# Sparse attention: scores from stacked split operands, with the causal mask as a matrix product and the keys spread by transfers

## The chip, the cores and the metric

One core of one Trainium2 chip runs the whole program. The metric is the time of one execution on the device, in microseconds (us). PE is TensorE (matrix products), DVE is VectorE, ACT is ScalarE, POOL is GpSimd, SP is SyncE, which here only issues loads of weights.

## What is computed

The program is a small network on 256 tokens of width 1024. Ten stages follow one another: a gated feed-forward block, an S5 mixer, two more feed-forward blocks, a convolution, a further feed-forward block, a retention layer, a mixture of experts by product keys ("peer"), a sparse attention ("nsa"), and a second peer. The change lies in the sparse attention alone. Cut to what matters, with 16 heads of 64 in 4 groups, so that four heads share keys and values:

```python
q = (h @ w_in)[..., :1024] * 64 ** -0.5
s = q . k_cmp                                  # coarse branch: 15 compressed keys
o_cmp = masked_softmax(s, end <= t) . v_cmp
s = q . k_slc ; o_slc = masked_softmax(s, tok <= t) . v_slc
s = q . k_win ; o_win = masked_softmax(s, kp <= t) . v_win
out = gate0 * o_cmp + gate1 * o_slc + gate2 * o_win
y = out @ w_o
```

With 256 tokens all blocks of 64 are selected and the window of 512 reaches over everything, so the second and the third branch are both full causal attention, with keys and values of their own.

## The kernel before, in words

Weights and activations are f32. A projection is done in three products of the type fp32r: each operand x is split into a high part (an ACT copy that rounds to fp32r) and a low part (DVE subtracts the high part), and high x high, high x low and low x high are added in PSUM (`mm3`, lines 281 to 283). Weights are loaded by SP, 1 MB each, into three buffers (`wload`, L247) and split by ACT and DVE (`wsplit`, L264, L265). The kernel uses eight PSUM banks: four under the tag "acc", two under "mm", two under "tr". Products outside the projections (scores, transposes, probabilities times values) take plain f32 operands.

The order of the instructions on each engine is made by a scheduler when the program is built: it takes what is ready by its own estimate of times, the earlier in the text first, and sets the waits. Work late in the text can so run early when its engine has nothing else; each engine then runs its list in order.

The stage `nsa` (L1395 to L1670) goes like this. Constants are loaded, among them the mask, [128, 2, 256]: 0 or -1e30 for each of two tiles of 128 queries. The values V of both branches are projected. Keys and values of the compressed branch go to `kv2` (L1427 to L1431), two copies for each of four groups, one of them a token ahead. Then `kT` (L1432 to L1442): for each branch b (two) the keys come from a projection into PSUM with two groups on the two row halves, and are copied, by ACT to rows 0 to 63 with zeros (POOL's memsets) in the other head slot, by DVE to rows 64 to 127 in the other slot. So one product of all 128 rows gives the scores of two heads side by side. `apply_pending` (L1444) finishes the layer norm of the stage before (eight DVE operations on 512 columns); the result is needed only at the end of this stage. The compression network follows (`nsfl`, L1458 to L1468), and the queries: `query(g)` (L1472 to L1475) projects four heads and copies them, scaled, into `qT`, two heads stacked on the row halves.

The attention loop (L1640 on) runs over 16 pairs of heads, eight pairs for the first query tile (one key tile of 128, so n = 128) and eight for the second (n = 256):

- `softmax(i)`: for both branches, one f32 product of q with `kT` into a bank "mm" (two heads x n columns, L1565); DVE adds the mask into `nssm` in SBUF (L1568); one DVE reduction over all gives the four negative maxima (L1571); ACT takes four exponentials in place, with their sums (L1574).
- `turn(i)`: PE transposes the probabilities (L1587), DVE and ACT copy them out (L1592, L1594).
- `attend(i)`: products with V (L1606), and after four pairs the scaling and summing into `o_sb`.

In the text `softmax` is two pairs ahead of `turn` and `attend`. `nssm` has three buffers. `coarse_softmax(qt)` and `coarse_out(qt)` do the compressed branch for a query tile; its scores are eight f32 products of 32 columns (L1515). Then come the output projection and the norm, and the next stage.

```python
def softmax(i):
    sm = nw.tile([P, 2, 2, S], F32, tag="nssm", bufs=3, ...)
    for b in range(2):
        sp = self.mm()
        nc.tensor.matmul(sp, lhsT=qT[:, g, fb, tile], rhs=kT[:, b, g, :, :n], start=True, stop=True)
        v.tensor_tensor(sm[:, b, :, :n], sp, mask[:, qt, :n], ALU.add)
    v.tensor_reduce(nm, sm[:, :, :, :n], AX.X, ALU.max, negate=True)
    ...
```

## Time and profile before

| what | us |
|---|---|
| median of 3 runs | 3199.64 (3199.46 to 3200.47) |
| the profiled execution | 3200.87 |
| its span, first to last instruction | 3199.1 |
| PE busy | 3120.6 |
| DVE busy | 2508.9 |
| ACT busy | 1567.3 |
| POOL busy | 105.0 |

The page of the profile gives busy time over the whole span. The stage `nsa` takes a small part of it, and is read in the views that take a stretch: a table by stretches, groups of instructions by line and shape, and a timeline. Product lengths on PE are pipelined (the next one starts before one has ended), so that their price is read from the distance of their starts.

### The profile page before, as it was taken

The page shows a single profiled execution, that of the slowest core. Times are in us where ns is not written, and L with a number is a line of the kernel's source. Part 1 is how long each engine was busy: PE and PEld are TensorE (multiplying, and loading weights), DVE is VectorE, ACT ScalarE, POOL GpSimd, SP SyncE. Part 2 cuts the span into 40 slices and gives each one's busy share as a digit, 9 for nine tenths or more (in the row PEclk, how much of TensorE's full clock was granted, in tenths as well). Part 3 has the DMA queues.
Part 4 walks back from the last instruction along what each step waited for, and adds up shares of the span by engine and source line. Part 5 has one row for each costly group of instructions (what it writes and reads, how often), then busy time and mean ns, then how long its engine had stood idle before and what let it go on. Part 6 is the DMA issues. An engine that isn't in the chain of part 4 may idle for free. (4 is left out here: it accounts for less than half of the span.)

```text
span 3199.1 us, 52281 instructions
## 1 busy us (share of the span) xinstructions
PE 3120.6 (98%) x20484; PEld 2829.5 (88%) x20484; DVE 2508.9 (78%) x4935; ACT 1567.3 (49%) x2350; POOL 105.0 (3%) x172
## 2 busy tenths in 40 slices
PE   8998999999999999999999999999999999999998
PEld 7888899898889888899999998888789999999887
DVE  8877867876986786899976666886789997666787
ACT  5556544446454443545654444335554665444432
POOL 1320000000000000000000000001000000000000
PEclk9999999999999999999999999999999999999999
DMA  5665767674266664445776666665044677566674
GB/s 212 209 230 184 290 228 278 242 287 146 89 242 244 251 250 169 168 153 200 231 255 214 215 215 212 228 226 194 32 159 160 206 235 258 201 215 215 211 239 163
DMA packets 174968, 668.36 MB, mean 209 GB/s; under 512 B 20705, under 2 KB 95233, under 8 KB 101762
## 3 DMA queue, kind: packets, MB, share of 16 engines
q1 hardware_dynamic: 150304, 606.05, 54.0%
q10 hardware_dynamic: 21826, 49.54, 4.1%
q0 software_dynamic: 2592, 9.44, 0.9%
q8 instruction: 161, 2.64, 0.3%
q14 instruction: 85, 0.70, 0.1%
HBM read 619.88 MB, written 45.11 MB: 208 GB/s over the span
## 5 line engine op out<-in xcount | busy, mean ns | idle before, releaser
L264 ACT ACTIVATE wh<-raw 128x1024 fp32r<-128x1024 f32 x948 | 998.5, 1059 | 1199.0 <-PE mm L282 617.6
L265 DVE TENSOR_TENSOR wl<-raw,wh 128x1024 fp32r<-128x1024 f32 x948 | 1150.1, 1221 | 403.9 <-ACT wh L264 392.9
L281 PE MATMUL mm<-xTh,wh 128*128 128x256 f32 x4032 | 1152.5, 286 | 4.5 <-ACT pg L1835 1.7
L283 PE MATMUL mm<-xTh,wl 128*128 128x256 f32 x4032 | 1142.5, 284 | 2.7 <-DVE wl L265 2.7
L282 PE MATMUL mm<-xTl,wh 128*128 128x256 f32 x4032 | 1144.5, 284 | 0.3 <-DVE xTl L355 0.3
L281 PEld LDWEIGHTS mm<-xTh,wh 128*128 128x128 f32 x4032 | 773.5, 192 | 15.7 <-ACT pg L1835 3.2
L282 PEld LDWEIGHTS mm<-xTl,wh 128*128 128x128 f32 x4032 | 773.6, 192 | 8.0 <-issue 0.7
L283 PEld LDWEIGHTS mm<-xTh,wl 128*128 128x128 f32 x4032 | 773.1, 192 | 4.7 <-DVE wl L265 4.4
L283 PE MATMUL acc<-wh,pal 128*128 128x512 f32 x1024 | 403.8, 394 | 0.0
L282 PE MATMUL acc<-wl,pah 128*128 128x512 f32 x1024 | 403.4, 394 | 0.0
L281 PE MATMUL acc<-wh,pah 128*128 128x512 f32 x1024 | 402.9, 393 | 0.0
L283 PEld LDWEIGHTS acc<-wh,pal 128*128 128x128 f32 x1024 | 192.6, 188 | 44.3
L281 PEld LDWEIGHTS acc<-wh,pah 128*128 128x128 f32 x1024 | 193.6, 189 | 39.3
L282 PEld LDWEIGHTS acc<-wl,pah 128*128 128x128 f32 x1024 | 192.7, 188 | 40.1
L1788 ACT ACTIVATE pwb<-tr 128x512 f32<-128x512 f32 x128 | 130.8, 1088 | 24.5 <-PE tr L1785 20.6
L281 PE MATMUL acc<-wh,gh 128*128 128x512 f32 x352 | 141.3, 402 | 0.0
L282 PE MATMUL acc<-wl,gh 128*128 128x512 f32 x352 | 139.8, 397 | 0.0
L283 PE MATMUL acc<-wh,gl 128*128 128x512 f32 x352 | 138.5, 399 | 0.3 <-DVE gl L405 0.3
L1781 DVE TENSOR_SCALAR poh<-pe_iota,pi,pwT 128x128 f32<-128x128 f32 x512 | 136.7, 338 | 0.0
L1849 DVE CAST pah<-pa 128x256 fp32r<-128x256 f32 x256 | 74.7, 293 | 69.6 <-PE acc L282 69.6
L1850 DVE TENSOR_TENSOR pal<-pa,pah 128x256 fp32r<-128x256 f32 x256 | 108.3, 424 | 25.3 <-DVE pah L1849 0.9
L1785 PE MATMUL tr<-poh,poh 128*128 128x128 f32 x1024 | 125.2, 275 | 1.6 <-ACT pwb L1788 1.6
(480 smaller groups left out, 3517.7 us busy)
## 6 DMA issues: line engine op xcount, KB each, us to landing
raw<-in_w SPq DMA_DIRECT2D x132, 1024.0 KB, 4.9
raw<-in_pe_u SPq DMA_DIRECT2D x128, 1024.0 KB, 4.8
raw<-in_pe_v SPq DMA_DIRECT2D x128, 1024.0 KB, 4.8
adaraw<-in_ada_w SPq DMA_DIRECT2D x48, 1024.0 KB, 6.9
pe_wscr<-pwb ACTq DMA_DIRECT2D x32, 1024.0 KB, 8.5
pwr<-pe_wscr SPq DMA_DIRECT2D x30, 1024.0 KB, 6.9
raw<-in_ret_vg SPq DMA_DIRECT2D x16, 1024.0 KB, 4.8
raw<-in_pe_wq SPq DMA_DIRECT2D x16, 1024.0 KB, 4.8
```

What stands on the lines that cost most here:

```text
L264: nc.scalar.activation(h, raw[:, sl], AF.Copy)
L265: nc.vector.tensor_sub(l, raw[:, sl], h.bitcast(F32))
L281: mm(out, lhsT=ah, rhs=bh, start=start, stop=False)
L282: mm(out, lhsT=ah, rhs=bl, start=False, stop=False)
L283: mm(out, lhsT=al, rhs=bh, start=False, stop=stop)
L1781: v.tensor_scalar(oh1[:, j, :], iota[:, :NK], i1[:, t:t + 1], wT[:, t:t + 1], ALU.is_equal, ALU.mult)
L1785: nc.tensor.matmul(ps[:, j * P:j * P + P], lhsT=oh2[:, t4 * 4 + j, :], rhs=oh1[:, t4 * 4 + j, :], start=True, stop=True)
L1788: nc.scalar.activation(wb[:, :, o:o + 4].rearrange("p i t -> p t i"), ps.rearrange("p (t i) -> p t i", t=4), AF.Copy)
L1849: v.tensor_copy(ah, a)
L1850: v.tensor_sub(al, a, ah.bitcast(F32))
```

## The change

- **Queries.** `qT` gets twice the room. For each head pair slot r (row half) ACT copies the scaled queries, rounded to fp32r, onto their own row half, and DVE writes the low part, scaled q minus high part, onto the other half. One column of 128 rows then holds a head's high and low part.
- **Keys.** The projected keys are split once over all 128 rows (`split_T`: one ACT copy, one DVE subtraction) into a high and a low part, and each of them is brought to both row halves by DMAs that POOL issues: 2 branches x 2 parts x 2 row halves read x 2 written, 16 of 128 KB. The copies and the memsets of `kT` go.
- **Scores.** For each head: queries x high keys (both branches side by side), then identity x mask on the last 128 keys of each branch, then queries x low keys, all fp32r and added in one PSUM bank. DVE reduces from PSUM; ACT's exponentials read PSUM and write SBUF.
- **Room.** `nssm` becomes three places: the two tiles of the stage's input (`new_T`, free after the last query) and one buffer. `kv2` lies in `o_sb`, which is written later.
- **Coarse scores**: sixteen fp32r products of 32 columns (high and low keys side by side) instead of eight f32 ones, and one more DVE addition.
- **Order.** `apply_pending` moves behind `query(1)`; `softmax(0)` moves ahead of `coarse_softmax(0)`. The mask shrinks to 128 x 128; ACT makes fp32r copies of it and of the identity.

```diff
-            mask, cmask = cload("ns_mask", [P, 2, S]), cload("ns_cmask", [P, 2, 2, 16])
+            cmask = cload("ns_cmask", [P, 2, 2, 16])
+            mask = np_.tile([P, P], F32, name="ns_mask")
+            nc.scalar.dma_start(out=mask, in_=self.I["ns_mask"][:, 0, :P])
...
-            kv2 = kp.tile([P, 2, 4, S], F32, name="ns_kv2")
+            kv2 = [o.rearrange("p h d -> p (h d)").rearrange("p (g t) -> p g t", g=4) for o in o_sb]
...
-            kT = np_.tile([P, 2, 4, 2, S], F32, name="ns_kT")
-            nc.gpsimd.memset(kT[0:64, :, :, 1, :], 0.0)
-            nc.gpsimd.memset(kT[64:128, :, :, 0, :], 0.0)
+            halves = [slice(0, 64), slice(64, 128)]
+            kT = [np_.tile([P, 4, 2, S], F32R, name="ns_kT" + i) for i in "hl"]
             for b in range(2):
                 ps = self.mm()
                 self.lin_b(xh, xl, self.I["ns_k"][b], ps)
-                for g in range(4):
-                    q = slice(64 * (g % 2), 64 * (g % 2) + 64)
-                    o = g // 2 * S
-                    nc.scalar.activation(kT[0:64, b, g, 0, :], ps[q, o:o + S], AF.Copy)
-                    v.tensor_copy(kT[64:128, b, g, 1, :], ps[q, o:o + S])
-
-            self.apply_pending()
+                parts = [nw.tile([P, 512], F32R, tag="nspT", bufs=4, name=self.nm("nsk")) for _ in range(2)]
+                self.split_T(ps, *parts)
+
+                for part, t in zip(parts, kT):
+                    for r, q in enumerate(halves):
+                        for d in halves:
+                            nc.gpsimd.dma_start(out=t[d, r::2, b, :], in_=part[q].rearrange("p (f t) -> p f t", f=2))
+
+            one = np_.tile([P, P], F32R, name="ns_one")
+            nc.scalar.activation(one, self.ident, AF.Copy)
+            low = np_.tile([P, 2, P], F32R, name="ns_low")
+            for b in range(2):
+                nc.scalar.activation(low[:, b, :], mask, AF.Copy)
...
-                nc.scalar.activation(qT[:, g].rearrange("p f t -> p (f t)"), ps, AF.Copy, scale=0.125)
+                for r, q in enumerate(halves):
+                    h, l = (qT[d, g, r].rearrange("p f t -> p (f t)") for d in (q, halves[1 - r]))
+                    nc.scalar.activation(h, ps[q], AF.Copy, scale=0.125)
+                    v.scalar_tensor_tensor(l, ps[q], 0.125, h.bitcast(F32), ALU.mult, ALU.subtract)
...
             query(1)
+            self.apply_pending()
...
-                for p in range(8):
-                    nc.tensor.matmul(cs[:, p * 32:p * 32 + 32], lhsT=qT[:, p // 2, p % 2, qt * P:qt * P + P],
-                                     rhs=kcT[:, p // 2].rearrange("p r n -> p (r n)"), start=True, stop=True)
+                for h in range(16):
+                    nc.tensor.matmul(cs[:, h * 32:h * 32 + 32], lhsT=qT[:, h // 4, h % 2, h % 4 // 2, qt * P:qt * P + P],
+                                     rhs=kcT[:, h // 4].rearrange("p i n -> p (i n)"), start=True, stop=True)
...
+                v.tensor_add(sc, sc, cs[:, :, 1, :])
...
+            rooms = [t.bitcast(F32).rearrange("p d t -> p (d t)")[:, :4 * S] for t in self.new_T()]
+            rooms.append(nw.tile([P, 4 * S], F32, tag="nssm", bufs=1, name=self.nm("nssm")))
...
-                sm = nw.tile([P, 2, 2, S], F32, tag="nssm", bufs=3, name=self.nm("nssm"))
-                for b in range(2):
-                    sp = self.mm()
-                    nc.tensor.matmul(sp[:, :2 * n].rearrange("p (r k) -> p r k", r=2),
-                                     lhsT=qT[:, g, fb, qt * P:qt * P + P],
-                                     rhs=kT[:, b, g, :, :n], start=True, stop=True)
-                    v.tensor_tensor(sm[:, b, :, :n], sp[:, :2 * n].rearrange("p (r k) -> p r k", r=2),
-                                    mask[:, qt, :n].unsqueeze(1).to_broadcast([P, 2, n]), ALU.add)
+                sm = rooms[i % 3]
                 nm = nw.tile([P, 2, 2], F32, tag="nsnm", bufs=3, name=self.nm("nsnm"))
-                v.tensor_reduce(nm, sm[:, :, :, :n], AX.X, ALU.max, negate=True)
                 for r in range(2):
+                    sp = self.mm()[:, :2 * n].rearrange("p (b k) -> p b k", b=2)
+                    q = qT[:, g, r, fb, qt * P:qt * P + P]
+                    nc.tensor.matmul(sp, lhsT=q, rhs=kT[0][:, g, :, :n], start=True, stop=False)
+                    nc.tensor.matmul(sp[:, :, n - P:], lhsT=one, rhs=low, start=False, stop=False)
+                    nc.tensor.matmul(sp, lhsT=q, rhs=kT[1][:, g, :, :n], start=False, stop=True)
+                    v.tensor_reduce(nm[:, r, :], sp, AX.X, ALU.max, negate=True)
                     for b in range(2):
-                        nc.scalar.activation(sm[:, b, r, :n], sm[:, b, r, :n], AF.Exp, bias=nm[:, b, r:r + 1],
+                        nc.scalar.activation(sm[:, b, r, :n], sp[:, b, :], AF.Exp, bias=nm[:, r, b:b + 1],
                                              accum_out=den[:, qt, 1 + b, h + r:h + r + 1])
...
-            coarse_softmax(0)
             softmax(0)
+            coarse_softmax(0)
             softmax(1)
```

## Rows read from the trace of the kernel before

**Rows 1.** The page, part 1: busy time of each engine over the span.

```profile
PE 3120.6 (98%) x20484; PEld 2829.5 (88%) x20484; DVE 2508.9 (78%) x4935; ACT 1567.3 (49%) x2350; POOL 105.0 (3%) x172
```

**Rows 2.** Table by stretches: each engine's busy us (instructions), PEclk, DMA share, GB/s.

```profile
2222.00:2248.00 26.00, 26.00 (x219) 25.81 (x216) 13.64 (x13) 15.69 (x21) 0.00 (x0) 1.00 0.66 243
...
2248.00:2320.00 72.00, 67.81 (x430) 53.85 (x428) 57.61 (x110) 42.48 (x154) 0.00 (x0) 1.00 0.04 15
```

**Rows 3.** Groups by shape, PE, 2181 to 2320: busy, mean ns | idle before, releaser.

```profile
L1565 PE MATMUL mm<-ns_kT,ns_qT 128*128 128x512 f32 x32 | 16.2, 600 | 0.3 <-DVE nssm L1568 0.2
...
L1565 PE MATMUL mm<-ns_kT,ns_qT 128*128 128x256 f32 x32 | 9.3, 399 | 1.2 <-DVE nssm L1568 1.1
```

**Rows 4.** Timeline of PE: start us, length us, instruction.

```profile
2245.00 0.28 PE L283 MATMUL mm<-xTh,wl 128*128 128x256 f32 x1
...
2245.12 0.28 PE L281 MATMUL mm<-xTh,wh 128*128 128x256 f32 x1
...
2301.96 1.88 PE L1565 MATMUL mm<-ns_kT,ns_qT 128*128 128x512 f32 x4
...
2303.68 1.89 PE L1606 MATMUL acc<-ns_V,nspT 128*128 128x64 f32 x16
...
2316.32 0.40 PE L282 MATMUL acc<-wl,oTh 128*128 128x512 f32 x1
...
2316.56 0.39 PE L283 MATMUL acc<-wh,oTl 128*128 128x512 f32 x1
```

**Rows 5.** Timeline of PE: the coarse products of the second query tile.

```profile
2255.70 1.87 PE L1515 MATMUL tr<-ns_kcT,ns_qT 128*128 128x32 f32 x16
```

**Rows 6.** Groups by shape, DVE: mask additions, reductions, and one out of PSUM (L1161).

```profile
L1568 DVE TENSOR_TENSOR nssm<-mm,ns_ns_mask 128x512 f32<-128x512 f32 x16 | 10.8, 684 | 2.3 <-PE mm L1565 2.0 <-PE tr L1587 0.2
...
L1571 DVE TENSOR_REDUCE nsnm<-nssm 128x4 f32<-128x1024 f32 x8 | 9.6, 1204 | 0.1
...
L1568 DVE TENSOR_TENSOR nssm<-mm,ns_ns_mask 128x256 f32<-128x256 f32 x16 | 6.4, 414 | 1.5 <-PE mm L1565 1.3
...
L1571 DVE TENSOR_REDUCE nsnm<-nssm 128x4 f32<-128x512 f32 x8 | 5.4, 678 | 0.1
...
L1161 DVE TENSOR_REDUCE adacol<-tr 128x4 f32<-128x512 f32 x28 | 18.2, 682 | 1.8 <-PE tr L1160 1.8
```

**Rows 7.** Groups by shape, ACT: exponentials, copies out of PSUM, the query copy.

```profile
L1574 ACT ACTIVATE nssm<-nssm,nsnm 128x256 f32<-128x256 f32 x32 | 15.8, 497 | 1.1 <-DVE nsnm L1571 1.0
...
L1574 ACT ACTIVATE nssm<-nssm,nsnm 128x128 f32<-128x128 f32 x32 | 12.4, 389 | 4.9 <-DVE nsnm L1571 4.9
...
L1594 ACT ACTIVATE nspT<-tr 128x256 f32<-128x256 f32 x8 | 3.0, 375 | 6.6 <-PE tr L1587 6.6
...
L1524 ACT ACTIVATE nssc<-nssc 128x256 f32<-128x256 f32 x2 | 0.8, 408 | 0.0
...
L1475 ACT ACTIVATE ns_qT<-mm 128x512 f32<-128x512 f32 x4 | 2.4, 588 | 1.0 <-PE mm L283 1.0
```

**Rows 8.** Instructions on the keys' tile: length ns (least, median, most), first and last start.

```profile
L1565 PE MATMUL mm<-ns_kT,ns_qT x64: 379/536/697, 2249.3 to 2308.8; 128*128 128x256 f32 x32, 128*128 128x512 f32 x32
...
L1441 ACT ACTIVATE ns_kT<-mm x8: 363/379/381, 2198.8 to 2209.3; 64x256 f32<-64x256 f32 x8
```

**Rows 9.** POOL's DMA issues; DMA sizes and us to landing; the stretch after the keys.

```profile
L312 POOL DMA_DIRECT2D rowbc<-in_ln_r x6 | 3.4, 568 | 621.8 <-ACT wh L264 619.1 <-ACT hT L340 2.8
...
rowbc<-in_ln_r POOLq DMA_DIRECT2D x6, 512.0 KB, 6.3
...
ns_cmp_w<-in_cmp_w ACTq DMA_DIRECT2D x1, 128.0 KB, 3.0
...
2199.00:2207.00 8.00, 8.00 (x72) 8.00 (x71) 3.65 (x9) 3.14 (x8) 0.00 (x0) 1.00 0.00 0
```

**Rows 10.** Table by stretches, columns as in rows 2: around an idle spot of PE.

```profile
2322.00:2324.00 2.00, 0.81 (x5) 0.61 (x5) 2.00 (x4) 1.65 (x2) 0.00 (x0) 1.00 0.03 8
...
2324.00:2326.00 2.00, 2.00 (x6) 1.58 (x5) 2.00 (x3) 2.00 (x3) 0.00 (x0) 0.52 0.00 0
```

More of the change, by code (lines that the diff above doesn't have):

```diff
@@ L1429, in nsa @@
                     o = g // 2 * S
-                    nc.scalar.activation(kv2[0:64, c, g, :], ps[q, o:o + S], AF.Copy)
-                    v.tensor_copy(kv2[64:128, c, g, 0:S - 1], ps[q, o + 1:o + S])
-            kT = np_.tile([P, 2, 4, 2, S], F32, name="ns_kT")
-            nc.gpsimd.memset(kT[0:64, :, :, 1, :], 0.0)
-            nc.gpsimd.memset(kT[64:128, :, :, 0, :], 0.0)
+                    nc.scalar.activation(kv2[c][0:64, g, :], ps[q, o:o + S], AF.Copy)
+                    v.tensor_copy(kv2[c][64:128, g, 0:S - 1], ps[q, o + 1:o + S])
+            halves = [slice(0, 64), slice(64, 128)]
+            kT = [np_.tile([P, 4, 2, S], F32R, name="ns_kT" + i) for i in "hl"]
             for b in range(2):
@@ L1448, in nsa @@
             nc.gpsimd.memset(hid, 0.0)
-            kcT = np_.tile([P, 4, 2, 16], F32, name="ns_kcT")
-            nc.gpsimd.memset(kcT, 0.0)
+            kcT = np_.tile([P, 4, 2, 16], F32R, name="ns_kcT")
+            nc.gpsimd.memset(kcT.bitcast(F32), 0.0)
             vc = np_.tile([P, 4, 64], F32, name="ns_vc")
@@ L1460, in nsa @@
                         fl = kp.tile([P, 4, 15], F32, tag="nsfl", bufs=4, name=self.nm("nsfl"))
-                        v.tensor_scalar(fl, kv2[:, c, :, 2 * lc:2 * lc + 225:16], pe[:, c, lc:lc + 1], None, ALU.add)
+                        v.tensor_scalar(fl, kv2[c][:, :, 2 * lc:2 * lc + 225:16], pe[:, c, lc:lc + 1], None, ALU.add)
                         for hb in range(2):
@@ L1469, in nsa @@
                                          AF.Gelu_apprx_tanh, bias=b1[:, c, hb:hb + 1])
-            qT = np_.tile([P, 4, 2, S], F32, name="ns_qT")
+            qT = np_.tile([P, 4, 2, 2, S], F32R, name="ns_qT")
             def query(g):
@@ L1486, in nsa @@
                 if c == 0:
-                    for half in range(2):
-                        nc.scalar.activation(kcT[64 * half:64 * half + 64, :, half, :15],
-                                             cp[:64, :P].rearrange("p (g n) -> p g n", g=4)[:, :, :15], AF.Copy)
+                    cpv = cp[:64, :P].rearrange("p (g n) -> p g n", g=4)[:, :, :15]
+                    for q in halves:
+                        nc.scalar.activation(kcT[q, :, 0, :15], cpv, AF.Copy)
+                    for q in halves:
+                        v.tensor_sub(kcT[q, :, 1, :15], cpv, kcT[:64, :, 0, :15].bitcast(F32))
                 else:
@@ L1513, in coarse_softmax @@
                 cs = self.tr()
-                for p in range(8):
-                    nc.tensor.matmul(cs[:, p * 32:p * 32 + 32], lhsT=qT[:, p // 2, p % 2, qt * P:qt * P + P],
-                                     rhs=kcT[:, p // 2].rearrange("p r n -> p (r n)"), start=True, stop=True)
+                for h in range(16):
+                    nc.tensor.matmul(cs[:, h * 32:h * 32 + 32], lhsT=qT[:, h // 4, h % 2, h % 4 // 2, qt * P:qt * P + P],
+                                     rhs=kcT[:, h // 4].rearrange("p i n -> p (i n)"), start=True, stop=True)
+                cs = cs.rearrange("p (h i n) -> p h i n", h=16, i=2)
                 sc = nw.tile([P, 16, 16], F32, tag="nssc", name=self.nm("nssc"))
                 sh = [P, 16, 16]
-                v.tensor_tensor(sc, cs[:, :S].rearrange("p (h n) -> p h n", h=16),
-                                cmask[:, 0, qt, :].unsqueeze(1).to_broadcast(sh), ALU.add)
+                v.tensor_tensor(sc, cs[:, :, 0, :], cmask[:, 0, qt, :].unsqueeze(1).to_broadcast(sh), ALU.add)
+                v.tensor_add(sc, sc, cs[:, :, 1, :])
                 mx = nw.tile([P, 16], F32, tag="nscm", name=self.nm("nscm"))
@@ L1555, in nsa @@
             pairs = [(qt, half, pr) for qt in range(NT) for half in range(2) for pr in range(4)]
+            rooms = [t.bitcast(F32).rearrange("p d t -> p (d t)")[:, :4 * S] for t in self.new_T()]
+            rooms.append(nw.tile([P, 4 * S], F32, tag="nssm", bufs=1, name=self.nm("nssm")))
+            rooms = [t.rearrange("p (b r k) -> p b r k", b=2, r=2) for t in rooms]
             def softmax(i):
@@ L1626, in nsa @@
             flat = [o.rearrange("p h d -> p (h d)") for o in o_sb]
+            softmax(0)
             coarse_softmax(0)
-            softmax(0)
             softmax(1)
```

## The prediction

> **What bounds the kernel now.** The page comes first: TensorE is busy 98% of the span, DVE 78%, ACT 49% [rows 1]. A busy PE is not yet PE at its peak, so the second view is the table by stretches. The change touches one stage, about 2181 to 2320 us. While the queries are projected (2222 to 2248) PE has no idle time, ACT 15.7 and DVE 13.6 us of work in 26. From there to 2320 PE is busy 67.8 of 72 us, so it idles 4.2, with DVE at 57.6 and ACT at 42.5 [rows 2]. PE therefore sets the time also in the attention loop, with DVE close behind. The third view, the groups by shape, says what the score products cost: 32 instructions of 512 columns and 32 of 256 (an f32 product is two instructions), and that PE idled 0.3 and 1.2 us before them, for DVE's mask additions [rows 3]. The mean of 600 ns there is a pipelined length and no price. The price is the distance of starts, in the timeline: four f32 instructions of 512 columns begin at 2301.96 and the next work at 2303.68, so 0.43 us each; one of 256 I take as half, 0.215. The products on split (fp32r) operands stand 0.235 us apart at 512 columns and 0.12 at 256; the small f32 products of the loop 0.118 (sixteen in 1.89) [rows 4].
>
> **The change part by part.**
> **Scores on PE.** Now: 32 x 0.43 + 32 x 0.215 = 20.6 us. After: for each of 16 pairs and 2 heads, two fp32r products and the mask product. With one key tile (8 pairs) all three have 256 columns: 48 x 0.12 = 5.8. With two (8 pairs) two have 512 and one 256: 16 x (2 x 0.235 + 0.12) = 9.4. Sum 15.2, so **5.4 us less PE work**. The products alternate weights as the projections behind [rows 4] do, so I see no reason for another price. Bounds: 4.4 (each of the 96 products 10 ns dearer) and 5.7.
> **Coarse scores.** Sixteen instructions per query tile take 1.87 us now [rows 5]; sixteen fp32r products of 32 columns replace them. At 0.117 each they are already at the distance of the small products, so 0, bounds -0.5 and +0.5. DVE gets one 256-wide addition more per tile, 2 x 0.41, beside PE.
> **DVE in the loop.** A pair now costs 2 x 0.684 + 1.204 = 2.57 us with two key tiles and 2 x 0.414 + 0.678 = 1.51 with one. After, two reductions out of PSUM: 512 wide from PSUM takes 0.682 where 512 from SBUF takes 0.678 [rows 6], so 1.36 and about 0.83. Over eight pairs each that is 15 us less of DVE. DVE is not the bound; only the waits that it causes count: 1.5 us of PE idle in [rows 3]. **I take -1.5**, bounds 0 and -2.7 (idle of 4.2 down to 1.5).
> **Exponentials out of PSUM.** ACT keeps 64 exponentials (0.389 at 128, 0.497 at 256). No row has the same one from PSUM; nearest are a copy of 256 from PSUM, 0.375, and an exponential of 256 from SBUF, 0.408, both without the sum [rows 7]. So I take no dearer, perhaps 0.03 cheaper. [...]
> What changes on the path is **how long a score buffer is held**. There are two PSUM buffers of this kind. Now each is free after DVE's addition. After, it is held until reduction and both exponentials are done, and what is queued behind it is everything on PE: next scores, then the product with V. With one key tile: after head 0's products, about 0.1 + 0.41 + 0.78 (head 0's exponentials) + 0.78 (head 1's) + 0.1 = 2.17 us until head 1's buffer is free, 1.81 after head 1's own products end. PE covers 12 small products x 0.118 + 0.36 = 1.78. So nothing is lost, or 0.4 us a pair where ACT's copy of the transposed probabilities (0.375) comes between. Over eight pairs: 0 to 3.2, **I take +1.0**, as ACT orders differ from pair to pair. With two key tiles: 0.1 + 0.68 + 1.0 + 1.0 + 0.1 - 0.59 = 2.3 against 24 x 0.118 + 0.59 = 3.4 of cover: no loss.
> **Queries.** Each goes from one ACT copy of 0.588 to two, plus two DVE operations 512 wide, nearest row 0.684 [rows 6, 7]: ACT +2.4, DVE +5.5 us in 26, where both had over 10 free [rows 2]: 0. The moved layer-norm application (eight DVE operations, about 5.4 us) runs ahead of this stage's copies now, when DVE has nothing else ready. I expect it there again; if it falls between the queries, DVE has 24.5 of 26, and the weight splits queue behind it. Bounds 0 and +1. After the last query the split is ready some 1.3 us later than the copy was; PE has head 0's first scores and the coarse products of three groups (0.36 + 1.4) in between, but head 1's scores wait for that query's buffer. **+0.7**, bounds 0 and +2.2.
> **Keys.** Eight ACT copies (0.379 each) and as many on DVE become one split per half, plus 16 transfers issued by POOL; POOL's two memsets go. Keys exist from 2198.8 on, all of them by 2209.3, and the first score product starts at 2249.3 [rows 8]. A POOL issue takes 0.57 us, so 16 take 9.1 on an idle engine; landing took 6.3 us at 512 KB, 3.0 at 128 KB on another queue; and from 2199 to 2207 the DMA engines stand idle [rows 9]. All are down by about 2222, with 27 us of cover. 2 MB more can delay the compression weights and the first query weights that follow: 0 to +1.5, **I take +0.5**.
> **Mask.** The load shrinks, three small ACT copies and a smaller memset: hidden in ACT's 10 free us.
> **Sum**: -5.4 - 1.5 + 1.0 + 0.7 + 0.5 = **-4.7 us**. The profiled execution took 3200.87 us (span 3199.1 and 1.8 around it), so 3196.2 for it; it stands 1.2 over the median of 3199.64, and against that median I forecast **3194.9**.
>
> **The rivals.**
> **More comes free.** If holding the buffers costs nothing and start and transfers stay hidden, PE's idle time of 4.2 falls to about 1.5, -5.4 - 2.7 = -8.1, 3191.5. For it: DVE's relief is three times the PE work saved. Against it: ACT becomes second in line, and its exponentials now release PE.
> **PE work was not the limit.** If idle time grows as PE work falls, the net is about -0.5: 3199. For it: with one key tile PE needs 2.14 us a pair, ACT 4 x 0.389 + 0.375 = 1.93, and the buffer about 2.2; all three are alike. Against it: half of the pairs have two key tiles, carry 4.3 of the 5.4 us, and have slack.
> [...]
> **The transfers come one at a time**, the opposite side: if each of the 16 waits for the landing of the one before (they write into two tiles), they need 16 x 3.0 = 48 us at the 128 KB row, and 16 x 6.3 = 101 at the 512 KB row, from 2200 on. The first scores wait at 2249, so it decides above 3.1 us each. At 4.0 the last lands at 2264, 15 us late: 3210. Against it: they write different partitions and rows.
>
> **How the numbers follow.** The forecast 0.45, more free 0.27, no limit 0.15, buffers 0.07, transfers 0.06. For this kernel 0.2%, 6.4 us, is about what a measurement can tell from no change: faster means under 3193.2, slower over 3206.0. Faster: the 0.27 and the fast edge of the forecast, 0.32. Slower: the transfers and the worst of the buffers, 0.08. Same: 0.60. The likeliest case alone reaches from 3192.5 to 3197.5; the range takes in the second and third case: 3190.8 to 3201.0, leaving the last two out, and the best ends of all bounds together.
>
> **What would show it.** Right: fp32r score products 0.235 and 0.12 us apart, about 15 us of them; DVE under 45 us in the 72; PE idle near 4. The first scores right behind the last query. Wrong: score products that start after an exponential with PE idle before them over 3 us in all (buffers); a wait of the first score product for a DMA (transfers); a granted clock under 1 between 2248 and 2320; score products at other distances; or a difference that lies outside this stage.

## The result and the profile after

The change made the kernel slower, by 0.5%: 3215.41 us (median of six runs, 3214.00 to 3216.47) against 3198.74 for the kernel before in the same session, ratio 1.0051 [1.0041, 1.0062]. The forecast was 3194.9. The profiled execution took 3214.86, 14.0 more than the one before (3200.87). Page of the kernel after, part 1, answering to [rows 1]:

```profile
PE 3129.8 (97%) x20516; PEld 2844.6 (89%) x20516; DVE 2501.8 (78%) x4925; ACT 1568.2 (49%) x2351; POOL 111.2 (3%) x186
```

PE was busy 9 us longer although its score products became cheaper. Cutting the stage at the starts of five products says where (the first of the compression network; the first of its second layer that takes the last result; the first score product; the first of 512 columns; the last product with V):

| stretch | before | after |
|---|---|---|
| compression | 16.9 | 25.7 |
| queries | 28.0 | 28.2 |
| loop, pairs with one key tile | 26.1 | 33.3 |
| loop, pairs with two | 46.6 | 42.1 |

The rest of the program adds 2.2; behind the loop, where no edit of this study reaches, the kept profiles differ by up to 3.4. So the largest loss, 8.8 us, lies ahead of the loop, in work that the diff hardly touches. Table by stretches, kernel after, columns as in [rows 2]:

```profile
2204.00:2208.00 4.00, 3.92 (x35) 3.79 (x34) 2.10 (x5) 1.95 (x4) 2.90 (x6) 1.00 0.93 182
2208.00:2210.00 2.00, 1.39 (x13) 1.39 (x13) 1.82 (x8) 0.66 (x3) 2.00 (x4) 1.00 1.06 206
2210.00:2234.00 24.00, 24.00 (x114) 23.24 (x114) 7.84 (x28) 5.38 (x15) 0.84 (x2) 0.50 0.57 181
2234.00:2248.00 14.00, 14.00 (x118) 13.99 (x117) 10.73 (x10) 10.61 (x13) 0.00 (x0) 1.00 0.68 254
...
2259.00:2264.00 5.00, 3.34 (x27) 3.07 (x25) 3.90 (x7) 3.75 (x10) 0.00 (x0) 1.00 0.57 200
2264.00:2276.00 12.00, 10.28 (x42) 8.70 (x41) 6.06 (x15) 5.08 (x21) 0.00 (x0) 0.57 0.02 6
...
2248.00:2320.00 72.00, 66.20 (x471) 60.20 (x470) 48.81 (x98) 41.44 (x144) 0.00 (x0) 0.93 0.13 45
```

Read the third row twice. PE is busy 24.00 of 24 us, so a busy column shows nothing wrong; the granted clock is 0.50. It fell 1.6 us behind the end of an idle spot of 0.69 us (rows one and two) and came back at 2234, 3.3 us after the stream of 60-column products had ended. The second fall, 0.57, is at the start of the loop.

**The idle spot.** Timeline of PE, kernel after:

```profile
2191.93 1.03 PE L329 MATMUL tr<-c_ident,z 128*128 128x128 f32 x8
2193.56 0.36 PE L281 MATMUL mm<-xTh,wh 128*128 128x256 f32 x1 [0.59 <-DVE ns_o L1435]
...
2205.14 2.79 PE L1473 MATMUL acc<-nsfl,raw 128*128 128x60 f32 x24
2208.61 9.90 PE L1473 MATMUL acc<-nsfl,raw 128*128 128x60 f32 x52 [0.69 <-DVE nsfl L1471]
```

and of DVE, the same stretch:

```profile
2206.18 0.27 DVE L1471 TENSOR_SCALAR nsfl<-ns_o,ns_cmp_pe 128x60 f32<-128x60 f32 x1 [0.17 <-PE acc L1473]
2206.37 0.67 DVE L405 TENSOR_TENSOR nsk<-mm,nsk 128x512 fp32r<-128x512 f32 x1
2206.97 1.27 DVE L344 TENSOR_TENSOR xTl<-hT,xTh 128x512 fp32r<-128x512 f32 x2
2208.17 0.95 DVE L1471 TENSOR_SCALAR nsfl<-ns_o,ns_cmp_pe 128x60 f32<-128x60 f32 x4
```

The small tile `nsfl` feeds the compression products and has four buffers. DVE's last one ends at 2206.45, the next starts at 2208.17: 1.7 us for the low part of the second branch's keys (0.67) and of the first token tile of the queries' input (1.27), which overlap a little. Now the kernel before, first PE, then DVE:

```profile
2206.56 0.28 PE L329 MATMUL tr<-c_ident,z 128*128 128x128 f32 x1
2206.68 0.55 PE L1463 MATMUL acc<-nsfl,raw 128*128 128x60 f32 x4
2207.07 0.94 PE L329 MATMUL tr<-c_ident,z 128*128 128x128 f32 x7
2208.02 5.57 PE L1463 MATMUL acc<-nsfl,raw 128*128 128x60 f32 x48
```

```profile
2205.73 0.27 DVE L1461 TENSOR_SCALAR nsfl<-ns_kv,ns_cmp_pe 128x60 f32<-128x60 f32 x1
2205.92 1.28 DVE L344 TENSOR_TENSOR xTl<-hT,xTh 128x512 fp32r<-128x512 f32 x2
2207.24 0.43 DVE L1442 COPY ns_kT<-mm 64x256 f32<-64x256 f32 x1
2207.70 0.81 DVE L1461 TENSOR_SCALAR nsfl<-ns_kv,ns_cmp_pe 128x60 f32<-128x60 f32 x4
```

DVE's gap was just as long there (2206.00 to 2207.70), and PE did not notice: eight transposes of the second token tile stood next on its list and filled it. After the change the scheduler has them 14.6 us earlier, at 2191.93. They stand as early in every kernel of this study that contains the change, with or without the transfers; which of the edits moved them was not traced.

**The start of the loop.** Timeline of PE, kernel after:

```profile
2258.92 0.28 PE L283 MATMUL mm<-xTh,wl 128*128 128x256 f32 x1
2259.04 0.28 PE L1589 MATMUL mm<-ns_kTh,ns_qT 128*128 128x256 f32 x1
...
2262.27 0.36 PE L1589 MATMUL mm<-ns_kTh,ns_qT 128*128 128x256 f32 x1 [1.16 <-DVE ns_qT L1488]
...
2263.57 0.39 PE L1589 MATMUL mm<-ns_kTh,ns_qT 128*128 128x256 f32 x1 [0.47 <-ACT xTh L1594]
...
2265.55 0.58 PE L1589 MATMUL mm<-ns_kTh,ns_qT 128*128 128x256 f32 x1 [0.66 <-ACT xTl L1594]
...
2267.50 0.58 PE L1589 MATMUL mm<-ns_kTh,ns_qT 128*128 128x256 f32 x1 [0.94 <-ACT xTl L1594]
```

and of ACT:

```profile
2259.24 0.59 ACT L1487 ACTIVATE ns_qT<-mm 64x512 fp32r<-64x512 f32 x1 [0.44 <-PE mm L283]
2260.81 0.59 ACT L1487 ACTIVATE ns_qT<-mm 64x512 fp32r<-64x512 f32 x1 [0.98 <-DVE ns_qT L1488]
2261.42 1.28 ACT L1594 ACT_TABLE_LOAD   x1
2262.71 0.37 ACT L1594 ACTIVATE xTh<-mm,nsnm 128x128 f32<-128x128 f32 x1
...
2265.39 1.05 ACT L264 ACTIVATE wh<-raw 128x1024 fp32r<-128x1024 f32 x1
2266.34 0.41 ACT L1541 ACTIVATE nssc<-nssc 128x256 f32<-128x256 f32 x1
```

The last query's split is a chain on one bank (ACT, DVE, ACT, DVE), 3.0 us from 2259.24 until PE resumes at 2262.27, and it holds one of the two score banks. The other three waits are for exponentials, and ahead of those stand on ACT's list the load of its table of exponentials (1.28), a weight split (1.05) and a coarse exponential (0.41). The four idle spots make 3.2 us. The clock falls at 2264.85, behind the first two of them, and is back at 2275.09.

**What came as forecast.** Timeline of PE, one pair with two key tiles:

```profile
2308.24 0.48 PE L1589 MATMUL mm<-ns_kTh,ns_qT 128*128 128x512 f32 x1
2308.55 0.28 PE L1590 MATMUL mm<-ns_low,ns_one 128*128 128x256 f32 x1
2308.67 0.40 PE L1591 MATMUL mm<-ns_kTl,ns_qT 128*128 128x512 f32 x1
...
2309.48 1.89 PE L1626 MATMUL acc<-ns_V,nspT 128*128 128x64 f32 x16
```

The two heads take 1.24 us (2308.24 to 2309.48), against four products of 0.43 in [rows 4]. The first product of a head can stand farther from the next than the 0.235 of the prediction, here 0.31.

### The profile page after: what moved, and what is told of

It is laid out like the page before. It is cut to its first block, busy times and chain, and to the rows that moved or that the text cites. A ratio compares the mean times of both kernels' runs of the same rounds, so it can differ in the third digit from the quotient of the medians.

```text
span 3213.1 us, 52392 instructions
## 1 busy us (share of the span) xinstructions
PE 3129.8 (97%) x20516; PEld 2844.6 (89%) x20516; DVE 2501.8 (78%) x4925; ACT 1568.2 (49%) x2351; POOL 111.2 (3%) x186
## 5 line engine op out<-in xcount | busy, mean ns | idle before, releaser
L281 PEld LDWEIGHTS mm<-xTh,wh 128*128 128x128 f32 x4032 | 773.4, 192 | 16.9 <-ACT pg L1855 3.2
L1808 ACT ACTIVATE pwb<-tr 128x512 f32<-128x512 f32 x128 | 130.7, 1088 | 25.7 <-PE tr L1805 20.6
L1869 DVE CAST pah<-pa 128x256 fp32r<-128x256 f32 x256 | 75.0, 294 | 69.9 <-PE acc L282 69.9
```

Source lines behind the costliest of these rows:

```text
L281: mm(out, lhsT=ah, rhs=bh, start=start, stop=False)
L1808: nc.scalar.activation(wb[:, :, o:o + 4].rearrange("p i t -> p t i"), ps.rearrange("p (t i) -> p t i", t=4), AF.Copy)
L1869: v.tensor_copy(ah, a)
```

## The experiments

Single runs of one kernel lie up to 7.7 us off their median, so beside the median with its ratio to the kernel before stand the stretches of one profiled execution, cut as above. No kernel leaves out a part of the computation.

| run | median us | ratio | compression | queries | loop |
|---|---|---|---|---|---|
| e1_ahead | 3206.61 | 1.0020 [1.0010, 1.0030] | 17.9 | 28.2 | 33.3 + 42.1 |
| e2_coarse_first | 3214.14 | 1.0046 [1.0032, 1.0060] | 26.1 | 30.6 | 31.6 + 42.0 |
| e3_four_score_banks | 3214.93 | 1.0051 [1.0034, 1.0068] | 25.5 | 28.4 | 32.9 + 42.1 |
| e4_before_short | 3214.67 | 1.0045 [1.0028, 1.0062] | 28.6 | 29.9 | 72.7 |
| e5_ahead_copies | 3200.93 | 1.0010 [1.0000, 1.0020] | 15.3 | 26.5 | 34.5 + 42.1 |
| e6_ahead_early | 3209.03 | 1.0031 [1.0021, 1.0041] | 17.8 | 107.7 with the loop | |
| e7_ahead_copies_early | 3205.81 | 1.0023 [1.0014, 1.0033] | 15.3 | 105.4 with the loop | |
| e8_copies_only | 3218.67 | 1.0056 [1.0041, 1.0072] | 29.5 | 27.8 | 75.8 |
| e9_start_four_banks | 3199.61 | 0.9999 [0.9990, 1.0008] | 15.3 | 26.5 | 32.6 + 42.1 |
| e10_start_banks_table | 3199.93 | 1.0000 [0.9991, 1.0009] | 15.3 | 26.5 | 30.8 + 42.1 |
| e11_coarse_late | 3196.95 | 0.9995 [0.9986, 1.0004] | 15.3 | 26.5 | 29.1 + 41.1 |
| e12_before_table | 3197.40 | 0.9992 [0.9983, 1.0001] | 16.9 | 28.0 | 25.2 + 45.5 |
| e13_one_bank | 3197.81 | 0.9994 [0.9985, 1.0003] | 15.3 | 26.5 | 26.4 + 43.3 |
| e14_one_bank_late | 3197.56 | 0.9992 [0.9983, 1.0001] | 15.3 | 26.5 | 26.0 + 45.7 |
| e15_held_transfers | 3205.86 | 1.0019 [1.0010, 1.0029] | 15.3 | 29.7 | 76.6 |
| e16_before_table_late | 3199.34 | 0.9996 [0.9987, 1.0005] | 17.0 | 28.0 | 26.2 + 45.5 |
| e17_one_bank_table_late | 3194.83 | 0.9987 [0.9978, 0.9996] | 15.3 | 26.5 | 24.2 + 45.7 |

### The compression: DVE's lead, and the transfers

**e1_ahead**, the kernel after with sixteen `nsfl`:

```diff
-fl = kp.tile([P, 4, 15], F32, tag="nsfl", bufs=4, name=self.nm("nsfl"))
+fl = kp.tile([P, 4, 15], F32, tag="nsfl", bufs=16, name=self.nm("nsfl"))
```

> The changed kernel with 16 instead of 4 buffers for the inputs of the compression products, so that DVE can write them ahead and PE does not wait for it; the order on PE stays the same but for two instructions. Theory 1 (an idle spot of 0.69 us before a compression product made the granted clock fall to 0.50, and the 60-column products kept it there for 24 us): no such wait, granted clock 1.00 from 2204 to 2234, the compression (first product to the first gate product) takes 16 to 17.5 us instead of 26.1, time 3206 +-1.5. Theory 2 (the 16 transfers with their small packets, which run in the same microseconds, brought the clock down or the products to a halt): the clock falls as before, time 3215 +-1.5.

PE's wait for DVE went, and half of the loss with it. What is left shows in the timeline of PE of this run, and in the stretches around it:

```profile
2203.75 10.38 PE L1473 MATMUL acc<-nsfl,raw 128*128 128x60 f32 x92
...
2216.25 5.42 PE L1473 MATMUL acc<-nsfl,raw 128*128 128x60 f32 x32 [0.96 <-DMA raw<-in_cmp_w]
```

```profile
2213.00:2217.00 4.00, 3.04 (x26) 2.70 (x25) 2.42 (x11) 0.43 (x2) 0.00 (x0) 1.00 1.37 286
2217.00:2225.00 8.00, 8.00 (x44) 7.68 (x44) 0.03 (x1) 2.60 (x8) 0.00 (x0) 0.57 0.66 255
```

Now a weight load is late: 0.96 idle, and the clock falls for the rest of the compression and 3 us beyond.

**e4_before_short**, the other way round: the kernel before, without a split score in it, with two `nsfl` (`bufs=4` to `bufs=2`).

> The kernel before with 2 instead of 4 buffers for the inputs of the compression products, so that PE has to wait for DVE there more often. Theory 1 (idle spots of half a microsecond or more among 60-column products bring the clock down and they cannot bring it up again): PE idle of 0.5 us or more in 2205 to 2222, granted clock 0.50 behind it, compression 6 to 10 us longer, time 3205 to 3209. Theory 2 (idle time there costs only itself): 0.5 to 2.5 us slower than the 3198.7 of the kernel before, granted clock 1.00 throughout.

It loses as much as the whole change does. Timeline of PE and stretches of this run:

```profile
2208.14 1.10 PE L1463 MATMUL acc<-nsfl,raw 128*128 128x60 f32 x8 [0.87 <-DVE nsfl L1461]
```

```profile
2210.00:2234.00 24.00, 23.84 (x114) 23.26 (x114) 9.88 (x30) 5.35 (x11) 0.00 (x0) 0.52 0.40 134
```

More than the 6 to 10 us that I expected. The idle spots of the whole compression make 1.3 us; the rest is the clock, which fell when 33 of the 128 products had started and stayed low for 27 us (in the kernel after it fell at 39, in e1 at 112). These two runs, taking the wait away and putting one in, show the cause of the compression's loss: the idle spot and the clock behind it.

**e5_ahead_copies**: e1 with engine copies in place of the sixteen transfers; **e8_copies_only**: the same with four `nsfl`.

```diff
-parts = [nw.tile([P, 512], F32R, tag="nspT", bufs=4, name=self.nm("nsk")) for _ in range(2)]
-self.split_T(ps, *parts)
...
-            nc.gpsimd.dma_start(out=t[d, r::2, b, :], in_=part[q].rearrange("p (f t) -> p f t", f=2))
+for r, q in enumerate(halves):
+    pv = ps[q].rearrange("p (f t) -> p f t", f=2)
+    for d in (q, halves[1 - r]):
+        nc.scalar.activation(kT[0][d, r::2, b, :], pv, AF.Copy)
+    for d in halves:
+        v.tensor_sub(kT[1][d, r::2, b, :], pv, kT[0][q, r::2, b, :].bitcast(F32))
```

> The kernel of e1 (16 buffers) with the 16 transfers replaced by copies of ACT (high parts) and subtractions of DVE (low parts) that write both row halves from PSUM. Theory 1 (in e1 the transfers held back the last load of compression weights, PE idled 0.96 us for it and the clock fell again): no wait of a compression product for a load, granted clock 1.00 from 2204 to 2234, compression 16 to 17 us, 2.5 to 4.5 us faster than e1's 3206.6, about 3203. Theory 2 (the load was late for another reason, or the engine copies cost what the transfers did): within 1.5 of 3206.6.

> The changed kernel with engine copies in place of the 16 transfers, and 4 buffers for the inputs of the compression products as it had. It tells which of the two, the transfers or DVE's lead, is enough alone. Theory 1 (DVE's lead decides): DVE, with 8 subtractions more in those microseconds, is late for a compression product again, by 0.5 us or more, the granted clock falls to 0.50, compression 24 us or more, 3212 to 3218. Theory 2 (the transfers decide): no fall before 2240, 3200 to 3205.

The transfers do cost something, 5.7 us between the medians of e1 and e5, more than expected; 4.3 of it shows in the compression and the queries (46.1 to 41.8). The fall of the clock went with the late load (in e5 it is 1.00 from 2202 to 2244). DMA issues from 2190 to 2260 (KB each, median us to landing), first e1, then e5:

```profile
raw<-in_cmp_w SPq DMA_DIRECT2D x2, 1024.0 KB, 8.7
```

```profile
raw<-in_cmp_w SPq DMA_DIRECT2D x2, 1024.0 KB, 4.8
```

But without the lead, nothing is gained by their going (e8): there PE waits 3.05 us for DVE's `nsfl`, and the clock is low for 27 us (0.50 from 2216 to 2240). So the first cause is DVE's lead, the second the transfers, and only one of them shows at a time.

**e15_held_transfers**: e1 with POOL's transfers behind small operations of POOL that need the last compression weight.

> The kernel of e1 (16 transfers, 16 buffers) with the transfers held until the last load of compression weights has landed (POOL writes one column of each key tile from that load before it issues them). It tells whether the transfers hurt by their time or at all. Theory 1 (they hurt only by standing beside that load): no wait of a compression product for a load, clock 1.00 in the compression, and the keys land by about 2232, ahead of the first scores: 3199.5 to 3202.5, as e5. Theory 2 (wherever they stand they delay a load of weights that PE needs): a wait for a load of query weights of 0.5 us or more, 3204 or more.

The compression was clean (15.3), the queries' loads were late instead. The waits of all engines, 2190 to 2250:

```profile
ACT wh L264 <- DMA raw<-in_ns_q: 4.5, 2, 3.4
```

Two of those loads took 9.2 and 11.0 us to land, 4.8 and 4.7 in e5. Moved, the transfers cross with the next weights, and the sum is the same.

### The order of the coarse scores, and an early pair

**e2_coarse_first** puts `coarse_softmax(0)` back ahead of `softmax(0)`:

```diff
-            softmax(0)
             coarse_softmax(0)
+            softmax(0)
```

> The changed kernel with the coarse scores of the first query tile ahead of the first pair's scores again, as in the kernel before. Theory 1 (the start of the loop is lost on two score buffers held until the exponentials are done, and on a clock that falls after it): PE idle between 2259 and 2269 stays at 3 to 4.5 us, time within 1.5 of 3215.4. Theory 2 (the moved first pair is the cause of the slow start): 3 to 5 us faster, 3211.

No gain: what the loop won (73.6 after 75.4), the queries lost, in a stretch that this edit does not touch. There the low clock of the compression lasted 5.9 us into the queries, 3.3 in the kernel after.

**e6_ahead_early** and **e7_ahead_copies_early** put pair 0's scores ahead of the last query, on e1 and on e5, with the second head of pairs 0 and 1 in an "acc" bank as in e3:

```diff
+            softmax(0)
             query(3)
...
-            softmax(0)
             coarse_softmax(0)
```

> The kernel of e1 with the scores and exponentials of pair 0 ahead of the last query's projection (its queries and keys exist by then; its probabilities go to the third buffer, which is free), and with the second head of pairs 0 and 1 in a bank of the kind acc. Theory 1 (the start is lost because PE has nothing but scores that wait for the last query, for ACT's table and for exponentials): PE idle in the first 15 us of the loop under 2 us where it was 3.3, no fall of the clock behind it, 5 to 8 us faster than e1's 3206.6: 3198.5 to 3201.5. Theory 2 (the two score buffers and ACT set the pace of pairs with one key tile anyway): the idle time moves behind, 3205 to 3207.

> e5 and e6 together. Theory 1: with both falls of the clock gone what remains is what the prediction had summed up, 3194 to 3197. Theory 2: 3203 or more.

Both missed: queries and loop together took 107.7 us after 103.6 in e1, and 105.4 after 103.1 in e5. Now, in e6, the last query's projection waits 1.70 us for the score bank that pair 0 holds; the wait was moved, and the clock fell twice there: the products of 256 columns start 0.21 us apart instead of 0.12 from 2247.9 to 2251.1, and again from 2258.3 on.

### The start of the loop: banks, table, order

**e3_four_score_banks**: the second head's scores of the first two pairs in "acc" banks, which are free then. **e9_start_four_banks**: both heads' scores of these pairs, on e5 (the edit below without `and r`).

```diff
-sp = self.mm()[:, :2 * n].rearrange("p (b k) -> p b k", b=2)
+sp = (self.acc() if i < 2 and r else self.mm())[:, :2 * n].rearrange("p (b k) -> p b k", b=2)
```

> The changed kernel where the second head of pairs 0 and 1 writes its scores into a bank of the other kind (acc), free at that time, so that the first four score groups do not wait for an exponential. Theory 1 (buffers held): the waits of score products for ACT's exponentials in the first 10 us of the loop (0.47 + 0.66 + 0.94) shrink below 0.7, and the fall of the clock at 2265 to 2275 goes or gets shorter: 2 to 6 us faster, 3209.5 to 3213.5. Theory 2 (the late last query and the loading of ACT's table set the start): the waits move to other places, time within 1 of 3215.4.

> The kernel of e5 (16 buffers, engine copies), with both heads of pairs 0 and 1 in the four banks of the kind acc. No score product of these pairs waits for the last query's bank or for an exponential. Theory 1 (waits for banks make the idle time at the start of the loop): the idle before score products in its first 15 us falls from 4.7 to under 2 us, the clock stays at 1.00 or falls for less than 6 us; 3 to 6 us faster than e5's 3200.9: 3195 to 3198. Theory 2 (ACT's chain of last query copies, table load of 1.28 us and exponentials makes it, and PE has nothing else to do): idle time the same within 1 us, the clock falls again, 3199.5 to 3201.5.

In neither was the clock saved (0.84 over the first half of the loop in both). The idle time of e9 stands in one place instead, in its list of waits of PE:

```profile
PE tr L1558 <- DVE nspc L1544: 3.1, 1, 3.1
```

The transposes of the coarse probabilities come next on PE's list, and they need the whole coarse softmax. **e10_start_banks_table** (on e9) adds an exponential of one column behind the gate's sigmoid, so that the table is loaded early; **e11_coarse_late** then moves the coarse work behind:

```diff
             nc.scalar.activation(gT, gp[:48, :S], AF.Sigmoid)
+            ex = kp.tile([48, 1], F32, name="ns_ex")
+            nc.scalar.activation(ex, gT[:, :1], AF.Exp)
...
-            coarse_out(0)
-            coarse_softmax(1)
...
+                if i == 0:
+                    coarse_out(0)
+                if i == 1:
+                    coarse_softmax(1)
```

> e9 with one exponential of a single column more, on the gates right behind their sigmoid, so that ACT's table of exponentials is loaded during the queries and not between the last query and the first pair. Theory 1 (both banks and table): PE idle in the first 15 us of the loop under 1.5 us, clock 1.00 there, 3193 to 3196. Theory 2 (ACT and DVE on the last query and the exponentials themselves set it): within 1 us of e9.

> The kernel of e10 with the coarse branch of the first query tile taken out behind the products with V of pair 0, and the coarse scores of the second tile behind pair 1, so that PE's list has the transposes of pair 0 where it had waited 1.8 us (e10) or 3.1 us (e9). Theory 1 (the idle time at the start is a matter of what stands next on PE's list; without it the clock stays up): idle of PE in the first 12 us of the loop under 2 us, clock 1.00 or down for less than 4 us, loop 69 to 71 us from the first score to the last product with V where e10 had 72.9, time 3195 to 3198. Theory 2 (ACT's exponentials pace the start whatever PE's order is): idle 2 us or more in one place, the clock falls for 8 us or more, 3199 to 3201.

In e10 the longest idle spot at the start is still 1.78 us, and the clock fell behind it for 7 us (0.89 over the first half); the loop took 72.9 after 74.7. With the coarse transposes out of the way (e11) the clock stayed at 1.00 through the loop; the loop took 70.2, with 29.1 in its first half after 30.8. The same two edits on the kernel before, **e12_before_table** (table alone) and **e16_before_table_late** (both):

> The kernel before with the one exponential more that loads ACT's table during the queries: what the remedy of e10 is worth where the clock did not fall. Theory 1 (idle time at the start that does not bring the clock down costs only itself): 0.5 to 1.3 us faster than 3199.9 at most, clock 1.00 in the loop. Theory 2 (the table is on no path there): within 0.4 us.

> The kernel before with the table and the late coarse branch of e11: what these remedies give without the split scores, so that e11 and e14 can be set against it. Theory 1 (split scores are worth 2 to 5 us once nothing brings the clock down): this one 3195.5 to 3198, slower than e14 by 1.5 us or more. Theory 2 (the split scores are worth nothing): within 1 us of e14 or faster.

With the table early the profiled loop is 2.0 us shorter there too, though not by the load's own time: in both, the first exponential starts 2.97 us after the first score, waiting for DVE's maxima. The median isn't told apart from no change. The later coarse work gave nothing there.

**e13_one_bank**: on e5, both heads of a pair with one key tile share one bank of 512 columns, reduced in one DVE operation. **e14_one_bank_late** does so on e11, **e17_one_bank_table_late** on e5 with the early table and the late coarse work.

```diff
+                sps = [self.mm()] * 2 if qt == 0 else None
                 for r in range(2):
-                    sp = self.mm()[:, :2 * n].rearrange("p (b k) -> p b k", b=2)
+                    sp = sps[r][:, r * S:r * S + S] if sps else self.mm()
...
+                    elif r:
+                        v.tensor_reduce(nm, sps[0].rearrange("p (r b k) -> p r b k", r=2, b=2), AX.X, ALU.max, negate=True)
```

> The kernel of e5 where a pair with one key tile has the scores of both heads side by side in one bank of 512 columns (one reduction of DVE for both), so that two pairs and not one fit into the two banks. Nothing else of the start is changed. Theory 1 (two banks held until the exponentials are done are the term that the prediction sized at 1.0 us, and bring the clock down): waits of score products for exponentials in the first half of the loop (about 3.5 us in e5) under 1.5 us, first half (first score to first score of 512 columns) 3 us or more shorter than e5's, 3196 to 3198.5. Theory 2 (the last query, the table and the place of the coarse transposes on PE's list start the loss; more banks only move the idle time): within 1.2 us of 3200.9, the clock falls again.

> The kernel of e11 with the one bank for each pair of e13. Theory 1 (with banks, table and list in order the change keeps what its arithmetic saves): first half of the loop 2 us or more shorter than in e11, second half unchanged, clock 1.00, 3193 to 3196. Theory 2 (ACT's exponentials pace the first half): first half within 0.7 us of e11's, 3196 to 3198.

> The best of what was found, without the borrowed acc banks of e14: 16 buffers, engine copies, one bank for each pair with one key tile in the two banks mm, the table loaded early, the coarse branch late. Theory 1: the stage (first copy of V to last product with V) takes 137.5 us or less, where the kernel before has 142.7 and e13 138.1, with the clock at 1.00 in the loop; 3194 to 3197, faster than the kernel before beyond its interval. Theory 2 (ACT's exponentials and the coarse branch pace the first half as in e14): stage 138 to 140 us, 3196.5 to 3198.5, not to be told from the kernel before.

One bank for a pair takes 8.1 us off the first half (34.5 to 26.4) and 6.9 off the loop (76.6 to 69.7), the largest single step in the loop: PE can run a whole pair ahead with the other bank. The second half got 1.2 longer in e13 and 3.6 in e14 and e17, as work moved over the border between the halves, so the whole loop is the measure. On e11, whose clock was up already, the one bank gave nothing: e14's loop took 71.7 after 70.2. Stretches at the start of the loop, e5, e13 and e17:

```profile
2244.00:2248.00 4.00, 2.65 (x22) 2.38 (x20) 2.96 (x5) 2.99 (x6) 0.00 (x0) 1.00 0.56 180
2248.00:2262.00 14.00, 12.06 (x45) 10.47 (x46) 7.30 (x18) 5.86 (x26) 0.00 (x0) 0.51 0.06 25
```

```profile
2252.00:2262.00 10.00, 9.74 (x61) 8.46 (x61) 6.35 (x14) 4.20 (x17) 0.00 (x0) 0.83 0.01 2
```

```profile
2250.00:2267.00 17.00, 15.46 (x105) 14.17 (x104) 12.38 (x30) 11.60 (x52) 0.00 (x0) 0.90 0.02 9
```

The clock there goes from 0.51 to 0.83 and 0.90. The stretches differ in length: counted from these means, with 0.50 as the lower level, it is low for 13.7 us of the 14 in e5, and for 3.4 in both others. e17 is the fastest kernel of the study; its interval does not reach 1, though at 0.13% it is inside the 0.2% named ahead. It is not told apart from e12, the kernel before with its table loaded early. Of the 3.9 us by which its profiled stage is shorter than that of e12, only 0.8 lie in the loop (69.9 against 70.7). The other 3.1 lie in the compression and the queries, 1.1 of them because the eight transposes stand ahead of the stretch. No run gives the kernel before sixteen `nsfl`, so these runs don't show that the split scores themselves made anything faster.

## Why the prediction was wrong

**The step that failed** is not a term of the sum but one that the sum lacks. The edits ahead of the loop were judged by when the keys are needed ("27 us of cover") and by the weight loads that they delay (+0.5). They were not judged by what they do to the order of the lists on which the compression stands. DVE's list gives PE four small tiles of lead and had its gap of 1.7 us before too; PE's list lost the eight transposes that had filled it. I took the unchanged part of the stage as a constant. That cost 8.8 of the 14.0 us: 0.69 idle and over 9 us of busy time at the lower clock, less 1.1 for the transposes, which now stand ahead of the stretch. e1 and e4 show the wait and the clock as the cause; that the moved transposes opened the wait is read from the timelines, and no run put them back.

**Scores on PE, -5.4: right in kind, at the low end of its bounds.** By the distance of starts a head takes 0.64 us with two key tiles (mean of the 14 heads without a wait in between) and 0.43 with one (8 heads), where I had 0.59 and 0.36; the f32 products before took 0.44 and 0.24. That saves about 3.8 and 0.7, 4.5 in all. The second half of the loop is 4.5 shorter too (42.1 after 46.6), but part of that is work that the first half had already done; in the first half the saving was lost in waits and in the clock.

**Coarse scores, 0: right.** Sixteen take 1.74 us in e11, where the clock stayed up, after 1.87.

**DVE's relief, -1.5: half right.** Its load in the 72 us fell from 57.6 to 48.8, not under 45; as eleven of these us are queries now, the fairer pair is the loop itself, 58.5 and 48.3. The waits for mask additions went. Waits for exponentials took their place, though "only the waits that it causes count" was the rule I had set myself.

**Held banks, +1.0, and late query, +0.7: too small, and without the clock.** Together with PE's saving of 1.1 they should have left the first half of the loop about level; it took 7.2 more. Over the whole loop PE idled 6.1 us after 4.4, where my terms (-1.5, +1.0, +0.7) made 4.6: 1.5 too little. Most of the rest is the clock: in the first half PE's busy time grew from 23.0 to 29.2, with the clock low for 10 us and some work drawn over from the second half. As to the waits, I had worked out the hold for the steady state, where PE has a product with V to cover it. At the start there is none: only coarse products stand between pairs 0 and 1. And I had counted only exponentials on ACT, not the table load, the weight split and the coarse exponential that stand between them. The query's split I took as 1.3 us later than the copy; ACT and DVE take turns on its bank, so it is 3.0 from the first copy's start until PE resumes, against one copy of 0.588 [rows 7]. That the held banks decide most of the loop's loss, with the clock that falls among their waits, is shown by e13: its loop is 6.9 shorter than that of e5.

In the trace of the kernel after, the waits at the start of the loop are idle pieces of 0.5 to 1.2 us between groups of score products, and the clock falls among them, 0.57 from 2264 to 2276.

**Transfers, +0.5: right in place, low in size.** They cross with the compression weights, whose last load took 9.5 us to land after 6.5; in the change itself the wait for DVE hides that, and with DVE's lead mended it is worth 5.7.

**Exponentials out of PSUM: right in sign.** Groups by shape, kernel after, ACT and DVE, against [rows 6, 7]:

```profile
L1594 ACT ACTIVATE xTh<-mm,nsnm 128x128 f32<-128x128 f32 x12 | 4.3, 365 | 2.1 <-DVE nsnm L1592 2.1
...
L1594 ACT ACTIVATE xTh<-mm,nsnm 128x256 f32<-128x256 f32 x12 | 5.6, 472 | 2.0 <-DVE nsnm L1592 2.0
```

```profile
L1592 DVE TENSOR_REDUCE nsnm<-mm 128x2 f32<-128x512 f32 x16 | 10.5, 685 | 2.1 <-PE mm L1591 2.0
```

In length these got 24 and 25 ns shorter (21 and 23 on the mean over all three places that they write to). From the start of one to the start of the next, with the reading of its sum between, the medians are 0.343 and 0.450 us where they were 0.385 and 0.492: 42 ns less. The 0.03 us that I had allowed for as "perhaps" lies between the 24 ns and the 42. The reduction is 7 ns longer than its like from SBUF.

**The rivals.** The buffers, at a chance of 0.07, had the mechanism of the loop's loss, waits for held banks and a fall of the clock. What a fall costs differs with the place: behind the loop in the kernel before, where products of 512 columns follow [rows 10], the granted clock is 0.53, 0.50, 0.50 and 0.76 in the four us from 2324 and 1.00 in the next; in the compression of the kernel after it is 0.50 for 24 us. "The transfers come one at a time" had the time nearest to the result (3210) by a wrong way: they overlap (POOL issued them 0.58 us apart, and they landed 2.8 and 3.8 us later, medians of the high and the low parts), and the first scores started 0.12 us behind the last query product. Of the signs that I had named as proof against me two came: scores behind exponentials with over 3 us of idle PE (3.5 in its list of waits), and a granted clock under 1 between 2248 and 2320 (0.93). No sign pointed at the compression.

**Open:** which edit made the scheduler move the transposes, and what exactly makes the clock fall.

## What to carry to other kernels

When work leaves an in-order list, look at what stands next to the place it leaves, on the engine that feeds and on the one that is fed: a gap that was covered may be open now. Price an idle spot of PE by what follows it: here the narrow products behind it ran at half the clock to their end, with PE 100% busy (0.50 granted, 24.00 of 24 us). So read the granted clock by stretches before the busy share. And where a buffer is held longer, work out the hold at the start of a loop, with all that stands on the engine which frees it.

## What was not expected of the hardware

Idle spots of 0.69, 0.87 and 0.96 us, each among products of 60 columns, were followed by a granted clock at the lower level until those products ended and 3 to 6 us more: for 24 us in the kernel after, 27 in e4, 7 in e1. An idle spot of 0.59 us ahead of products of 256 columns in the kernel after (it ends at 2193.56) was followed by no fall, the clock being 1.00 from 2193 to 2204, nor was one of 2.04 us among them in e15 (2236.73 to 2238.76; 1.00 from 2234 to 2250).

The length of an idle spot alone does not decide in these traces. Behind the loop, ahead of the output projection, ten of them (before, after, e2, e3, e9, e10 and e14 to e17) show one of 1.20 to 1.27 us in the same place. The products of 512 columns behind it soon start 0.43 us apart in three (before, after and e14; the granted clock is 0.52 from 2324 to 2326 in the first [rows 10] and from 2338 to 2340 in the second), and stay at 0.23 in the other seven.

Where the clock was low and PE full, it stayed low with 60-column products (0.50 from 2210 to 2234 in the kernel after) and was 1.00 again from 2234 on, when products of 256 columns had come (from 2231.25 on).
